# Interleaving the two halves of split weights: stationary operands at every second word

## The chip, the cores and the metric

One NeuronCore of a Trainium2 chip runs the whole kernel. The metric is the time of one execution on the device in microseconds. A profile of one execution lies beside it: each instruction's start and recorded duration by engine, the DMA transfers, and the clock that TensorE was granted.

## The reference, cut to what matters

One encoder layer over 256 tokens of width 2048, in fp32:

```
hn   = rmsnorm(x) * norm_w
q, v, f_fwd, f_bwd, z_a, b_gate, c_gate, h_b, z_b = split(hn @ w_in, 9)   # 2048 -> 9 x 2048
o_a  = head_rmsnorm(hgrn2_bidirectional(silu(q), v, f_fwd, f_bwd)) * silu(z_a)
o_b  = rmsnorm(b_gate * conv3(c_gate * h_b)) * silu(z_b)
h    = x + concat(o_a, o_b) @ w_out                                       # 4096 -> 2048
h    = h + (p @ w_ple) * sigmoid(h @ w_ple_gate)
out  = rmsnorm(h) * final_norm_w
```

The change touches the first product alone, `hn @ w_in`, whose weights are 2048 x 18432.

## The kernel before, in words

**Exactness.** TensorE multiplies fp32r operands. To keep fp32 exactness each operand is split in two: `hi` is the value rounded to fp32r, `lo` is what is left of it. A product is then hi x hi + hi x lo + lo x hi, summed in PSUM.

**Weights.** `Stream` (from line 31) brings them in. A DMA on SP's queue fills a `raw` tile of 128 x 2048 words (three buffers), which makes two units of 1,024 words per partition. For each unit `open` (line 58) takes one of five `spl` tiles of 128 x 2048 words, and `split` (line 68) fills it in two instructions: ScalarE casts `raw` to `hi` (line 69), VectorE subtracts `hi` from `raw` and writes `lo` (line 70). In the tile the 256 `hi` words of a k-tile lie next to each other, and its 256 `lo` words behind them; the view `[partition, k, s, n]` names them with s = 0 for `hi` and s = 1 for `lo`. `get` (line 72) keeps three units split ahead of the one in use.

**The GEMM.** A block is 256 columns of `w_in` for all 16 k-tiles, four units of four k-tiles. There are 72 blocks. Stage A runs i = 0 to 7 over FF, FB, Q, ZA, V (line 523), with the recurrence of two heads between the matmuls; stage B runs i = 0 to 7 over CG, HB, BG, ZB (line 547). ZA and V are token-major (16 blocks): x is the stationary operand, the weight the moving one. The other 56 are column-major: the weight is the stationary operand, x (`xs`) the moving one. For each k-tile and each half m of 128 columns `gemm_part` (line 272) issues a pair:

```
lh, ll = w[:, k, 0, m * P : (m + 1) * P], w[:, k, 1, m * P : (m + 1) * P]       # line 281
rf, rh = xs[:, kt, :, :].rearrange("p s n -> p (s n)"), xs[:, kt, 0, :]         # line 282
pe.matmul(a[:, :T], lhsT=ll, rhs=rh, start=False, stop=False)                   # line 287
pe.matmul(a, lhsT=lh, rhs=rf, start=False, stop=(kt == NKT - 1))                # line 288
```

The first takes `lo` of the weight as stationary operand and moves 256 columns, the second takes `hi` and moves 512 (for the first k-tile the two come the other way round, lines 284 and 285). So a block is 32 pairs, and each matmul has its own load of 128 stationary columns. After a block `evac` (line 297) adds the two halves of the accumulator, ScalarE at line 307 and VectorE at line 308; accumulators lie in four PSUM buffers, two for a block.

**Order.** Each engine takes its instructions in program order. The first two blocks (FF and FB of i = 0) have an order written out by hand (from line 317); behind them the tile framework orders the engines, and `at`/`tick` (lines 212 to 221) put the recurrence's matmuls (lines 459, 501, 511, 512) between k-tiles.

Of the kernel before, what the change touches and what calls it, by code (L numbers as in the profile page):

```python
# [25 lines left out]
B_Q, B_V, B_FF, B_FB, B_ZA, B_BG, B_CG, B_HB, B_ZB = (8 * i for i in range(9))  # L26
# [4 lines left out]
class Stream:  # L31


    def __init__(self, nc, rawp, splp, ahead):
        self.nc, self.rawp, self.splp, self.ahead = nc, rawp, splp, ahead
        self.todo = []
        self.where = []
        self.raws = {}
        self.parts = {}
        self.next = 0  # L40

    def add(self, src):

        j = len(self.todo)
        _, k, n = src.shape
        self.todo.append((src, k, n))
        first = len(self.where)
        self.where += [(j, h) for h in range(k * n // 1024)]
        return list(range(first, len(self.where)))
# [8 lines left out]
    def open(self, i):  # L58
        j, h = self.where[i]
        n = self.todo[j][2]  # L60
        if j not in self.raws:
            self.load(j)
        half = self.raws[j][:, h * 1024 : (h + 1) * 1024].rearrange("p (k n) -> p k n", n=n)
        part = self.splp.tile([P, 2048], F32R, tag="spl", name=f"spl{i}")
        self.parts[i] = part.rearrange("p (k s n) -> p k s n", s=2, n=n)
        return half, self.parts[i]

    def split(self, r, v):
# [12 lines left out]
def tile_hymba_encoder(  # L81
# [33 lines left out]
    ws = Stream(nc, rawp, splp, 3)  # L115

    blocks = {}
    for i in range(8):
        for c in (B_FF, B_FB, B_Q, B_ZA, B_V):
            blocks[c, i] = sum((ws.add(w_in[c + i, h]) for h in range(2)), [])  # L120
    for i in range(8):
        for c in (B_CG, B_HB, B_BG, B_ZB):
            blocks[c, i] = sum((ws.add(w_in[c + i, h]) for h in range(2)), [])
    oblocks = [sum((ws.add(w_out[j, h]) for h in range(8)), []) for j in range(4)]
    gblocks, pblocks = [], []
    for j, (c0, n) in enumerate(GCOLS):
# [660 lines left out]
```

## Time and profile before

| | |
|---|---|
| median of 3 runs | 1158.66 us (1158.42 to 1159.83) |
| the profiled execution | 1158.74 us |
| its span, first to last instruction | 1157.0 us |
| TensorE: matmul busy, weight loads busy | 1142.3 us, 981.4 us |
| VectorE, ScalarE, GpSimd busy | 763.6, 639.9, 234.8 us |
| mean granted TensorE clock | 0.995 of full |
| read from HBM | 211.11 MB |

In the profile PE is TensorE's matmuls and PEld its weight loads, which overlap the matmuls; DVE is VectorE, ACT is ScalarE, POOL is GpSimd, SP the queue that issues the DMAs. A group of instructions is named by line, engine, operation and tiles, out<-in, with the count after x. Recorded durations of successive matmuls overlap, so that their starts tell more than their durations.

### The profile page before, as it was taken

The numbers are of one execution on the slowest core, as the hardware profiler recorded it, in microseconds if no ns is written. First come the engines' busy times: TensorE is split into PE (matmuls) and PEld (weight loads), VectorE is DVE, ScalarE is ACT, GpSimd is POOL, SyncE is SP. The second block draws the span as 40 slices with busy tenths as digits, with TensorE's granted clock in tenths as the row PEclk, the third lists the DMA queues.
The fourth block names the chain that finished last, engine by engine and source line by source line (L and its number), as shares of the span: only waits on it lengthen the run. The fifth ranks groups of instructions, "written<-read, shape, count | busy, mean of one in ns | idle before, by whom it ended". The sixth has DMA issues, their size and how long they took to land.

```text
span 1157.0 us, 16851 instructions
## 1 busy us (share of the span) xinstructions
PE 1142.3 (99%) x6832; PEld 981.4 (85%) x6832; DVE 763.6 (66%) x949; ACT 639.9 (55%) x889; POOL 234.8 (20%) x167
## 2 busy tenths in 40 slices
PE   8999999999999999999999999999999999999997
PEld 7878888888888888888888888888888888888886
DVE  6687777685958585966666666676666545545554
ACT  6767576666758584855544444444444334434554
POOL 1232414151414041331221221121210000000121
PEclk9999999999999999999999999999999999999999
DMA  8754545454544555455555555555557555555541
GB/s 284 301 175 153 183 163 196 152 183 146 198 167 159 174 177 181 152 178 182 183 187 184 198 191 187 182 182 184 187 190 262 183 198 180 191 204 196 197 166 74
DMA packets 31614, 214.29 MB, mean 185 GB/s; under 512 B 3504, under 2 KB 3888, under 8 KB 7088
## 3 DMA queue, kind: packets, MB, share of 16 engines
q1 hardware_dynamic: 31392, 213.14, 53.6%
q8 instruction: 53, 0.87, 0.3%
q14 instruction: 25, 0.20, 0.1%
q10 hardware_dynamic: 144, 0.08, 0.0%
HBM read 211.11 MB, written 2.10 MB: 184 GB/s over the span
## 4 chain that ended last, share of the span: by engine, by line
PE 93%; DVE 2%; DMA 2%; POOL 1%; ACT 1%; SPq 0%; issue 0%; ACTq 0%; DVEq 0%
PE a L288 41%; PE a L287 21%; PE a L284 3%; PE pa L630 3%; PE pb L630 3%; PE pb L631 3%; PE pb L632 3%; PE pa L631 3%; PE pa L632 3%; PE pg L630 3%; PE pg L631 3%; PE pg L632 3%; PE a L285 1%; DVE spl L70 1%; PE scps L459 1%; PE cx L501 1%
## 5 line engine op out<-in xcount | busy, mean ns | idle before, releaser
L70 DVE TENSOR_TENSOR spl<-raw,spl 128x1024 fp32r<-128x1024 f32 (+1 forms) x389 | 522.3, 1348 | 305.9 <-ACT spl L69 304.9
L288 PE MATMUL a<-xs,spl 128*128 128x512 f32 x1680 | 597.2, 398 | 0.0
L69 ACT CAST spl<-raw 128x1024 fp32r<-128x1024 f32 (+1 forms) x389 | 405.0, 1045 | 343.0 <-PE a L288 193.7
L287 PE MATMUL a<-xs,spl 128*128 128x256 f32 x1680 | 476.0, 283 | 0.5 <-DVE spl L70 0.3
L288 PEld LDWEIGHTS a<-xs,spl 128*128 128x128 f32 x1680 | 316.7, 189 | 73.0
L287 PEld LDWEIGHTS a<-xs,spl 128*128 128x128 f32 x1680 | 318.1, 189 | 3.7 <-DVE spl L70 1.3
L288 PE MATMUL a<-spl,xs 128*128 128x512 f32 x480 | 171.4, 401 | 2.2 <-DVE spl L70 2.2
L287 PE MATMUL a<-spl,xs 128*128 128x256 f32 x480 | 135.4, 282 | 0.0
L288 PEld LDWEIGHTS a<-spl,xs 128*128 128x128 f32 x480 | 91.0, 190 | 24.1 <-DVE spl L70 2.5
L287 PEld LDWEIGHTS a<-spl,xs 128*128 128x128 f32 x480 | 91.4, 190 | 0.7
L307 ACT COPY r<-a 128x256 f32<-128x256 f32 x112 | 40.6, 372 | 47.4 <-PE a L288 46.8
L691 POOL TENSOR_TENSOR hh<-hh,fw 128x512 f32<-128x512 f32 (+1 forms) x10 | 12.8, 1293 | 264.5 <-PE pp L632 245.0
L630 PE MATMUL pg<-spl,ht 128*128 128x512 f32 (+1 forms) x160 | 55.7, 348 | 0.0
L632 PE MATMUL pg<-spl,ht 128*128 128x512 f32 (+1 forms) x160 | 55.5, 347 | 0.0
L631 PE MATMUL pg<-spl,ht 128*128 128x512 f32 (+1 forms) x160 | 55.5, 347 | 0.0
L630 PE MATMUL pa<-spl,mixa 128*128 128x512 f32 x128 | 51.2, 400 | 0.0
L438 POOL TENSOR_TENSOR qc<-pf,ge 128x256 f32<-128x256 f32 x16 | 43.9, 2748 | 34.4 <-DVE pf L430 34.4
L631 PE MATMUL pb<-spl,mixb 128*128 128x512 f32 x128 | 50.6, 395 | 0.0
L630 PE MATMUL pb<-spl,mixb 128*128 128x512 f32 x128 | 50.6, 395 | 0.0
L632 PE MATMUL pb<-spl,mixb 128*128 128x512 f32 x128 | 50.6, 395 | 0.0
L631 PE MATMUL pa<-spl,mixa 128*128 128x512 f32 x128 | 50.6, 395 | 0.0
L632 PE MATMUL pa<-spl,mixa 128*128 128x512 f32 x128 | 50.6, 395 | 0.0
(174 smaller groups left out, 1233.7 us busy)
## 6 DMA issues: line engine op xcount, KB each, us to landing
raw<-in_w_in_dram SPq DMA_DIRECT2D x140, 1024.0 KB, 5.0
raw<-in_w_out_dram SPq DMA_DIRECT2D x32, 1024.0 KB, 4.9
raw<-in_w_gate_dram SPq DMA_DIRECT2D x12, 1024.0 KB, 4.9
raw<-in_w_gate_end_dram SPq DMA_DIRECT2D x4, 1024.0 KB, 4.9
raw<-in_w_in_dram SPq DMA_DIRECT2D x7, 512.0 KB, 8.4
xf<-in_xtok_dram SPq DMA_DIRECT2D x1, 2048.0 KB, 9.9
hh<-in_xtok_dram SPq DMA_DIRECT2D x1, 2048.0 KB, 8.8
raw<-in_w_ple_dram SPq DMA_DIRECT2D x4, 512.0 KB, 3.5
```

The source lines that it names most:

```text
L69: self.nc.scalar.copy(out=v[:, :, 0, :], in_=r)
L70: self.nc.vector.tensor_tensor(out=v[:, :, 1, :], in0=r, in1=v[:, :, 0, :], op=ALU.subtract)
L284: pe.matmul(a, lhsT=lh, rhs=rf, start=True, stop=False)
L285: pe.matmul(a[:, :T], lhsT=ll, rhs=rh, start=False, stop=False)
L287: pe.matmul(a[:, :T], lhsT=ll, rhs=rh, start=False, stop=False)
L288: pe.matmul(a, lhsT=lh, rhs=rf, start=False, stop=(kt == NKT - 1))
L307: act.copy(out=r, in_=acc[m][:, 1, :])
L438: pool.tensor_tensor(out=c64(dst[:, d]), in0=c64(src[:, d, :, half * P : (half + 1) * P]), in1=g.unsqueeze(3).broadcast_to([P, 2, 2, CH]), ...
L630: pe.matmul(acc[m], lhsT=lh, rhs=w[:, k, 0, :], start=(kt == 0), stop=False)
L631: pe.matmul(acc[m], lhsT=lh, rhs=w[:, k, 1, :], start=False, stop=False)
L632: pe.matmul(acc[m], lhsT=ll, rhs=w[:, k, 0, :], start=False, stop=(kt == nk - 1))
L691: pool.tensor_tensor(out=h, in0=h, in1=fw[:, cs], op=ALU.mult)
```

## The change

The units of 23 blocks are laid out otherwise in their `spl` tile: `hi` and `lo` of each weight lie side by side, so that a view of `hi` alone, or of `lo` alone, steps by two words (8 bytes). These are FB for i = 1 to 7 and HB and ZB for all i, all of them column-major. The instructions and their order stay; ScalarE writes `hi` at this step, VectorE reads `hi` and writes `lo` at it, and TensorE loads its stationary operands at it.

```diff
     def __init__(self, nc, rawp, splp, ahead):
...
+        self.side = []
...
-    def add(self, src):
+    def add(self, src, side=False):
...
         self.todo.append((src, k, n))
+        self.side.append(side)
...
     def open(self, i):
...
         part = self.splp.tile([P, 2048], F32R, tag="spl", name=f"spl{i}")
-        self.parts[i] = part.rearrange("p (k s n) -> p k s n", s=2, n=n)
+        form = "p (k n s) -> p k s n" if self.side[j] else "p (k s n) -> p k s n"
+        self.parts[i] = part.rearrange(form, s=2, n=n)
...
     for i in range(8):
         for c in (B_FF, B_FB, B_Q, B_ZA, B_V):
-            blocks[c, i] = sum((ws.add(w_in[c + i, h]) for h in range(2)), [])
+            blocks[c, i] = sum((ws.add(w_in[c + i, h], c == B_FB and i > 0) for h in range(2)), [])
     for i in range(8):
         for c in (B_CG, B_HB, B_BG, B_ZB):
-            blocks[c, i] = sum((ws.add(w_in[c + i, h]) for h in range(2)), [])
+            blocks[c, i] = sum((ws.add(w_in[c + i, h], c in (B_HB, B_ZB)) for h in range(2)), [])
```

## Rows read from the trace of the kernel before

**Rows 1.** The page: busy time of each engine, and TensorE's clock by slices.
```profile
PE 1142.3 (99%) x6832; PEld 981.4 (85%) x6832; DVE 763.6 (66%) x949; ACT 639.9 (55%) x889; POOL 234.8 (20%) x167
...
PEclk9999999999999999999999999999999999999999
```

**Rows 2.** Waits of TensorE for the GEMM: us in total, times, longest.
```profile
PE a L288 <- DVE spl L70: 2.2, 1, 2.2
...
PE a L287 <- DVE spl L70: 0.3, 1, 0.3
```

**Rows 3.** The page: the chain that ended last, by engine, by line.
```profile
PE 93%; DVE 2%; DMA 2%; POOL 1%; ACT 1%; SPq 0%; issue 0%; ACTq 0%; DVEq 0%
PE a L288 41%; PE a L287 21%; PE a L284 3%; PE pa L630 3%; PE pb L630 3%; PE pb L631 3%; PE pb L632 3%; PE pa L631 3%; PE pa L632 3%; PE pg L630 3%; PE pg L631 3%; PE pg L632 3%; PE a L285 1%; DVE spl L70 1%; PE scps L459 1%; PE cx L501 1%
```

**Rows 4.** Column-major groups by form: busy us, mean ns | idle before.
```profile
L288 PE MATMUL a<-xs,spl 128*128 128x512 f32 x1680 | 597.2, 398 | 0.0
...
L287 PE MATMUL a<-xs,spl 128*128 128x256 f32 x1680 | 476.0, 283 | 0.5 <-DVE spl L70 0.3
...
L287 PEld LDWEIGHTS a<-xs,spl 128*128 128x128 f32 x1680 | 318.1, 189 | 3.7 <-DVE spl L70 1.3
L288 PEld LDWEIGHTS a<-xs,spl 128*128 128x128 f32 x1680 | 316.7, 189 | 73.0
```

**Rows 5.** Timeline of TensorE in ZB, i = 1: start us, us, what.
```profile
585.11 0.28 PE L287 MATMUL a<-xs,spl 128*128 128x256 f32 x1
...
586.52 0.28 PE L287 MATMUL a<-xs,spl 128*128 128x256 f32 x1
586.64 0.40 PE L288 MATMUL a<-xs,spl 128*128 128x512 f32 x1
586.88 0.28 PE L287 MATMUL a<-xs,spl 128*128 128x256 f32 x1
...
591.82 0.28 PE L287 MATMUL a<-xs,spl 128*128 128x256 f32 x1
...
594.30 0.28 PE L287 MATMUL a<-xs,spl 128*128 128x256 f32 x1
```

**Rows 6.** Weight loads by form: the recurrence's loads of 32 columns.
```profile
L459 PEld LDWEIGHTS scps<-pf,dd 128*32 128x32 f32 x384 | 10.4, 109 | 0.0
```

**Rows 7.** Timeline of weight loads: six in a row between short matmuls.
```profile
216.85 0.19 PEld L512 LDWEIGHTS o<-vt,sx 128*128 128x128 f32 x1
...
217.40 0.19 PEld L287 LDWEIGHTS a<-xs,spl 128*128 128x128 f32 x1
```

**Rows 8.** Timeline of TensorE in CG, i = 1.
```profile
550.39 0.28 PE L287 MATMUL a<-xs,spl 128*128 128x256 f32 x1
...
560.45 0.28 PE L287 MATMUL a<-xs,spl 128*128 128x256 f32 x1
```

**Rows 9.** The split's two groups, by form.
```profile
L70 DVE TENSOR_TENSOR spl<-raw,spl 128x1024 fp32r<-128x1024 f32 x387 | 520.9, 1352 | 304.8 <-ACT spl L69 303.7
L69 ACT CAST spl<-raw 128x1024 fp32r<-128x1024 f32 x387 | 403.8, 1047 | 341.8 <-PE a L288 193.7 <-PE pb L632 56.1 <-PE pa L632 47.1
```

**Rows 10.** Small VectorE groups: stepped operands (line 422), contiguous ones (199).
```profile
L422 DVE TENSOR_TENSOR gx<-dd,pf 128x6 f32<-128x6 f32 x8 | 1.3, 159 | 0.0
...
L199 DVE TENSOR_TENSOR et<-vec,mx 128x32 f32<-128x32 f32 x2 | 0.3, 190 | 0.0
```

**Rows 11.** Stage B by window: us, busy PE, PEld, DVE, ACT, POOL, clock, DMA.
```profile
600.00:700.00 100.00, 100.00 (x569) 86.92 (x568) 65.40 (x73) 46.92 (x61) 20.24 (x14) 1.00 0.56 189
```

**Rows 12.** Timeline, both engines of one split for ZB, i = 1.
```profile
580.74 1.05 ACT L69 CAST spl<-raw 128x1024 fp32r<-128x1024 f32 x1 [1.77 <-PE a L288]
...
581.82 1.23 DVE L70 TENSOR_TENSOR spl<-raw,spl 128x1024 fp32r<-128x1024 f32 x1 [1.60 <-ACT spl L69]
```

**Rows 13.** The page: DMA issues, KB each, median us to landing.
```profile
raw<-in_w_in_dram SPq DMA_DIRECT2D x140, 1024.0 KB, 5.0
```

## Prediction

> **What bounds the kernel now.** I read the busy shares first. TensorE has a matmul in flight 99% of the span, and its granted clock is at the full level (2.4 GHz) in practically every slice; VectorE and ScalarE are busy 66% and 55% [rows 1]. A busy TensorE does not yet prove that TensorE is the limit, so the waits come next: in the whole span the longest wait of a matmul of this GEMM for a split is 2.2 us, once, and the next is 0.3 us [rows 2]. The chain of waits says the same: 93% of it is TensorE, and 62 points of that are the two matmul lines 287 and 288 [rows 3]. What counts, then, is not how busy anything is, but how far apart two matmuls start. That is read from a timeline of TensorE alone, because the recorded durations overlap: a 512-column matmul is recorded with 398 ns and a 256-column one with 283 ns [rows 4], but the first starts of 27 successive pairs in ZB, i = 1, a block that the change touches, lie 594.30 - 585.11 = 9.19 us apart, 26 steps of 0.353 us [rows 5]. Within a pair the 256-column matmul holds the array for 0.12 us and the 512-column one for 0.23 to 0.24 us [rows 5]. The weight load of each matmul (189 ns recorded, [rows 4]) starts with the matmul before it and so lies beside that one.
>
> So the place to look at is the 0.12 us of the 256-column matmul: the load of the next `hi` operand has to fit in there.
>
> **The change part by part.**
>
> *How much is touched.* Side by side are FB for i = 1 to 7 (7 blocks) and HB and ZB for i = 0 to 7 (16): 23 of the 56 column-major blocks, 23 of all 72. A block is 16 k-tiles x 2 halves = 32 pairs, so 736 pairs, that is 1,472 weight loads at a step of 8 bytes, and 23 x 4 = 92 splits. Instruction counts, DMAs, queues, the order of the work and all semaphores stay as they are; nothing is added or moved.
>
> *Weight loads.* No row of the trace has a stationary operand with a step, so the cost is bounded from both sides. The low end is zero. For the high end I take that every column takes twice as long to come in. What a column costs follows from two rows: a load of 128 columns takes 189 ns [rows 4], one of 32 columns 109 ns [rows 6], so 96 columns take 80 ns, 0.83 ns each, 107 ns for 128, and 82 ns are fixed. How closely loads can follow each other is seen where short matmuls leave nothing else to wait for: six loads in a row, the first at 216.85 and the last at 217.40 with two merged rows of two between them, are 0.55 / 5 = 0.11 us apart [rows 7]. Under the 256-column matmul (0.12 us) there is thus about 0.01 us to spare, under the 512-column one 0.12 us. Twice the time per column adds 0.107 us: under the 512-column matmul it stays hidden (0.22 against 0.23), under the 256-column one 0.10 us of it comes out. High end: 736 x 0.10 = 74 us.
> Between 0 and 74 us I take zero, by the row that is nearest. While the loads bring in a column each 0.83 ns, the moving operand, of the same fp32r type and out of SBUF too, is read at 512 columns in 0.235 us [rows 5], 0.46 ns each. A load at every second word spans 256 words in 107 ns, 0.42 ns for each word passed over: the pace at which the moving operand already passes over its words. Reading past every second word asks of the memory about what the engine gets from it for the other operand.
> The Trainium skill has a price for this, SBUF — State Buffer, section "Door 1: The DMA port swizzle" (its box on cachelines): lines of 16 bytes, full bandwidth from two hits in a line on. At 8 bytes a line is hit twice instead of four times, so the sum by that page is 0 us as well; no run here shows it yet, and two hits is the least that it allows.
>
> *A gain from the loads.* This is not excluded either, since the same pair runs at two paces in this trace: in CG, i = 1, 29 steps from pair to pair take 560.45 - 550.39 = 10.06 us, 0.347 us a pair [rows 8], with the same shapes, the same clock and the same operands' layout as the 0.353 us of [rows 5]. If the new loads tipped all 736 pairs to the quicker pace, it would be 736 x 0.0066 = 4.9 us. In the other direction, the longest steps of [rows 5] (0.12 and 0.24 us) for every pair would be 0.36, 736 x 0.0065 = 4.8 us more. I take neither: 0.
>
> *Splits.* ScalarE writes 1,024 values with a step, VectorE reads one operand and writes its result with a step. Today they take 1,047 and 1,352 ns in the mean [rows 9]. The only rows with a stepped operand on VectorE are small: six values at a step of 256 bytes take 159 ns, 32 contiguous ones 190 ns [rows 10], 26 values more for 31 ns; so the step makes no value visibly dearer, though six are few. Bounds: nothing, and twice the present time. I take nothing; and up to the high end it is covered. In 100 us of stage B VectorE works 65.4 us and ScalarE 46.9 us [rows 11]; 100 us hold 35 units of 2.83 us, half of them side by side, so twice the time adds 17.7 x 1.23 = 22 us and 17.7 x 1.05 = 19 us: 87 and 66 us, still below 100. The cover that hides the latency is the lead: the split that ends on VectorE at 583.05 [rows 12] is first used by the matmul at 591.82 [rows 5], 8.8 us later. ScalarE started it right after a matmul of line 288 gave its buffer free [rows 12], so the lead comes from the five buffers, and a chain slower by 1.05 + 1.23 us leaves 6.5 us of it. Queued behind the longer splits on these engines are the evacuations (lines 307, 308); an accumulator is wanted again one block, some 11 us, after its last matmul, so a few us of delay there stop nobody. Behind VectorE's splits waits SP's queue too, which loads a `raw` tile again once both its halves are split; three tiles are six units, 17 us, and a transfer lands after 5.0 us [rows 13], so 1.23 us more are covered there as well. If the cover were gone, TensorE would wait at the first matmul of a unit.
>
> *Sum.* 0 + 0 + 0. The profiled execution took 1158.74 us (span 1157.0 and 1.7 around it), 0.1 us above the median of the runs, so I predict **1158.7 us**. A measurement of this kernel tells about 0.2% (2.3 us) from no change.
>
> **Rivals.**
> 1. *The stepped load is slower* (the other side). Place: the load under the 256-column matmul, 736 times. It decides from 0.01 us on, 12 columns' worth. At twice the time per column +74 us, **1232 us**; at one and a half times 0.053 - 0.01 = 0.043 us x 736, +32 us, **1190 us**. For it: the cover there is nearly used up already, and no row shows such a load. Against it: the pace of the moving operand. Chance 0.15, two thirds of it near the high price. The same box of the skill's page says that each access that crosses to a new line pays a penalty, without a figure; taken alone, that sentence would speak for this rival.
> 2. *The pairs fall into another pace.* For it: 0.347 and 0.353 us stand side by side for equal work [rows 5, 8], so the pace hangs on something fine, which the load's timing could be. Quicker: -4.9 us, **1153.8 us**, chance 0.14. Slower: +4.8 us, **1163.5 us**, chance 0.06. Against both: 0.353 us is the common pace; 569 matmuls in 100 us of stage B [rows 11] are 0.352 us a pair.
> 3. *The splits outgrow their cover.* Stage B has 100 - 65.4 = 34.6 us of VectorE left per 17.7 units, so a split may grow by 1.95 us to about 3.2 us; only past that does VectorE set the pace. At three times today's time (2.46 us more) it would be 0.5 us for each of the 92 splits, 47 us, **1206 us**. For it: nothing seen. Chance 0.03.
>
> **How the numbers follow.** No visible effect 0.62. Faster is rival 2's quick half, 0.14. Slower is 0.15 + 0.06 + 0.03 = 0.24. From 1153.5 to 1164.5 us lie the forecast and both halves of rival 2, 0.82; left out are rivals 1 and 3.
>
> **What would show it.** Right: pairs in HB and ZB at 0.353 us as in CG and BG, loads still near 189 ns, no more waits of TensorE for splits than now. Wrong by rival 1: loads of lines 284 to 288 longer in the touched blocks alone, and the step after a 256-column matmul 0.2 us instead of 0.12. By rival 2: touched blocks at another length than their neighbours with loads unchanged. By rival 3: long splits, and TensorE waiting for line 70 in stage B. If ScalarE's or VectorE's splits grow and the time does not, the cover was as reckoned.

## The result, and the profile after

| | before | changed |
|---|---|---|
| median | 1159.24 us (1158.42 to 1160.18) | 1153.59 us (1152.67 to 1154.78) |
| ratio | | 0.9949 [0.9936, 0.9961] |
| the profiled execution | 1158.74 us, span 1157.0 us | 1154.37 us, span 1152.7 us |
| mean granted clock | 0.995 | 0.996 |

Both medians are over four runs. The changed kernel is faster by 0.51%. The forecast was no visible effect, 1158.7 us: the gain was missed, and the measured time lies just inside the lower edge of the range (1153.5 us). In the changed kernel every line behind the inserted ones has a number 4 higher: the pair is 291 and 292, the split 73 and 74.

The page of the changed kernel, with the rows that answer to [rows 1, 3]: busy time, clock, chain.

```profile
PE 1136.3 (99%) x6832; PEld 985.1 (85%) x6832; DVE 762.6 (66%) x949; ACT 647.7 (56%) x889; POOL 235.0 (20%) x167
...
PEclk9999999999999999999999999999999999999998
...
PE 93%; DVE 2%; DMA 2%; POOL 1%; ACT 1%; SPq 0%; issue 0%; ACTq 0%; DVEq 0%
```

The page says where to look, and no more: the count of instructions is the same, TensorE still bounds the kernel with the same 93% of the chain, and its matmuls are busy 6.0 us less. Its waits for splits, as in [rows 2]:

```profile
PE a L292 <- DVE spl L74: 2.7, 1, 2.7
...
PE a L291 <- DVE spl L74: 0.3, 1, 0.3
```

No wait went away: the two are as they were, one of them 0.5 us longer. So 5 us were not won from a stall; the matmuls themselves follow each other faster. The groups by form, as in [rows 4, 9]:

```profile
L292 PE MATMUL a<-xs,spl 128*128 128x512 f32 x1680 | 591.9, 395 | 0.0
L74 DVE TENSOR_TENSOR spl<-raw,spl 128x1024 fp32r<-128x1024 f32 x387 | 519.9, 1349 | 307.1 <-ACT spl L73 306.2
L291 PE MATMUL a<-xs,spl 128*128 128x256 f32 x1680 | 474.5, 282 | 0.4 <-DVE spl L74 0.3
L73 ACT CAST spl<-raw 128x1024 fp32r<-128x1024 f32 x387 | 412.1, 1069 | 335.5 <-PE a L292 173.8 <-PE pb L636 56.1 <-PE pa L636 47.4
L291 PEld LDWEIGHTS a<-xs,spl 128*128 128x128 f32 x1680 | 322.7, 192 | 3.3 <-DVE spl L74 1.0
L292 PEld LDWEIGHTS a<-xs,spl 128*128 128x128 f32 x1680 | 321.2, 191 | 63.7
```

The loads went up by 2 to 3 ns in the mean, the matmuls down by 1 to 3 ns, and ScalarE's casts up by 22 ns. A mean over touched and untouched blocks hides what each does. (Touched blocks are the 23 with side-by-side units; a load at the step of 8 bytes is called stepped below.) So the next view is the loads of one touched block alone, ZB of i = 1 (583 to 593 us):

```profile
L292 PEld LDWEIGHTS a<-xs,spl 128*128 128x128 f32 x30 | 5.9, 195 | 1.0
L291 PEld LDWEIGHTS a<-xs,spl 128*128 128x128 f32 x29 | 5.7, 196 | 0.0
```

and of the untouched block ahead of it, BG of i = 1 (572 to 582 us):

```profile
L291 PEld LDWEIGHTS a<-xs,spl 128*128 128x128 f32 x29 | 5.4, 188 | 0.0
L292 PEld LDWEIGHTS a<-xs,spl 128*128 128x128 f32 x29 | 5.4, 188 | 1.3
```

A stepped load takes 7 to 8 ns more. The kernel got faster with dearer loads. The timeline of TensorE shows where: the start of stage B's second round, the two blocks just named with their first and last pairs, and the first matmul behind the GEMM.

```profile
548.70 0.40 PE L288 MATMUL a<-xs,spl 128*128 128x512 f32 x1
...
571.02 0.40 PE L288 MATMUL a<-xs,spl 128*128 128x512 f32 x1
...
571.73 0.28 PE L291 MATMUL a<-xs,spl 128*128 128x256 f32 x1
...
581.78 0.28 PE L291 MATMUL a<-xs,spl 128*128 128x256 f32 x1
...
582.13 0.39 PE L288 MATMUL a<-xs,spl 128*128 128x512 f32 x1
...
583.19 0.28 PE L291 MATMUL a<-xs,spl 128*128 128x256 f32 x1
583.31 0.40 PE L292 MATMUL a<-xs,spl 128*128 128x512 f32 x1
583.54 0.28 PE L291 MATMUL a<-xs,spl 128*128 128x256 f32 x1
...
592.99 0.28 PE L291 MATMUL a<-xs,spl 128*128 128x256 f32 x1
593.34 0.40 PE L288 MATMUL a<-xs,spl 128*128 128x512 f32 x1
...
861.99 0.48 PE L634 MATMUL pa<-spl,mixa 128*128 128x512 f32 x1
```

The touched block runs 28 steps in 592.99 - 583.19 = 9.80 us, 0.350 us a pair, where the same block took 0.353 [rows 5]. The untouched block runs 29 steps in 581.78 - 571.73 = 10.05 us, 0.347 us a pair: the quicker of the two paces that were there before [rows 5, 8].

K-tile by k-tile the start times show what a pace is. A quick block takes 0.693 to 0.694 us for each k-tile, two pairs. At the slow pace the k-tiles take about 0.715, 0.704 and 0.701 us in turn, so that 0.353 us is the mean of a pattern of three k-tiles. The touched blocks take 0.700 us for each. A block of Q, ZA or stage B (i from 1 on) has one pace from its fourth k-tile on. In an unstepped one the second k-tile already tells which: 0.711 to 0.712 us in all that go on slowly, 0.698 to 0.700 us in all that go on quickly, in both traces. So in these two kernels the pace of a block is settled at its start.

Two points of the kernel before enclose the same stretch (timeline of TensorE, CG of i = 1 and the first matmul behind the GEMM):

```profile
549.69 0.40 PE L284 MATMUL a<-xs,spl 128*128 128x512 f32 x1
...
866.34 0.48 PE L630 MATMUL pa<-spl,mixa 128*128 128x512 f32 x1
```

866.34 - 549.69 = 316.65 us before, 861.99 - 548.70 = 313.29 us after: 3.36 us won over 28 blocks. From block start to block start in the two timelines, each of the 14 touched ones (HB and ZB) is 0.07 to 0.08 us shorter and each of 13 untouched ones (CG and BG) 0.18 us; the fourteenth, CG of i = 1, had the quick pace already [rows 8]. 14 x 0.075 + 13 x 0.18 = 3.4 us. Over all 72 blocks the touched ones won 1.34 us (FB 0.24, HB 0.63, ZB 0.47) and the untouched ones 4.2 us (Q 1.27, ZA 0.51, CG 0.99, BG 1.44); the start of the kernel (the first two blocks, V of i = 0 and FF of i = 1) took 1.2 us more, which makes 4.36 us. Q and CG (from i = 1 on) and every BG stand directly behind a touched block. ZA does not: it follows Q, and only ZA of i = 2, 4 and 6 won. Behind the GEMM both take 290.7 us. **Three quarters of the gain lie in blocks that the change doesn't touch.**

A count of matmuls in 100 us of stage B serves for the experiments; the columns are those of [rows 11], where it is 569:

```profile
600.00:700.00 100.00, 100.00 (x575) 88.73 (x574) 66.17 (x73) 49.32 (x62) 18.97 (x14) 1.00 0.56 189
```

### The profile page after: what moved, and what is told of

Read it like the earlier page. It is cut to its first block, busy times and chain, and to the rows that moved or that the text cites. A ratio compares the mean times of both kernels' runs of the same rounds, so it can differ in the third digit from the quotient of the medians.

```text
span 1152.7 us, 16851 instructions
## 1 busy us (share of the span) xinstructions
PE 1136.3 (99%) x6832; PEld 985.1 (85%) x6832; DVE 762.6 (66%) x949; ACT 647.7 (56%) x889; POOL 235.0 (20%) x167
## 4 chain that ended last, share of the span: by engine, by line
PE 93%; DVE 2%; DMA 2%; POOL 1%; ACT 1%; SPq 0%; issue 0%; ACTq 0%; DVEq 0%
PE a L292 40%; PE a L291 21%; PE a L288 3%; PE pa L634 3%; PE pb L636 3%; PE pb L634 3%; PE pa L636 3%; PE pb L635 3%; PE pa L635 3%; PE pg L636 3%; PE pg L635 3%; PE pg L634 3%; PE a L289 1%; PE scps L463 1%; DVE spl L74 1%; PE cx L505 1%
## 5 line engine op out<-in xcount | busy, mean ns | idle before, releaser
L73 ACT CAST spl<-raw 128x1024 fp32r<-128x1024 f32 (+1 forms) x389 | 413.3, 1066 | 335.8 <-PE a L292 173.8
L292 PEld LDWEIGHTS a<-xs,spl 128*128 128x128 f32 x1680 | 321.2, 191 | 63.7
L291 PEld LDWEIGHTS a<-xs,spl 128*128 128x128 f32 x1680 | 322.7, 192 | 3.3 <-DVE spl L74 1.0
```

Of the source, the lines that this page charges most:

```text
L73: self.nc.scalar.copy(out=v[:, :, 0, :], in_=r)
```

## The experiments

### Loads or splits: which half of the change does it

Each kernel steps one side alone, in the change's 23 blocks. In the first, the tiles are written without a step and read with one:

```diff
 # e1_loads, in open()
-        return half, self.parts[i]
+        return half, part.rearrange("p (k s n) -> p k s n", s=2, n=n)
 # e2_writes, in open(); self.parts[i] keeps the old form
-        return half, self.parts[i]
+        return half, part.rearrange(form, s=2, n=n)
```

> Loads stepped, splits contiguous, in the same 23 blocks (the touched stationary operands mix hi and lo words, so the product of these blocks is another one). Theory P (the stepped loads shift the phase between loads and matmuls, and a block entered in another phase runs at 0.347 us a pair instead of 0.353): as the changed kernel, 1153.6 us, with CG and BG at 10.88 us from first to last matmul start. Rival W (the stepped writes of ScalarE and VectorE do it, by their own timing or their traffic): as before, 1159.2 us, CG and BG at 11.05 us.

> Splits stepped, loads contiguous, in the same 23 blocks (the touched stationary operands mix hi and lo words, so the product of these blocks is another one). Theory P: as before, 1159.2 us, CG and BG at 11.05 us, loads at 189 ns. Rival W: as the changed kernel, 1153.6 us, CG and BG at 10.88 us.

Stepped loads alone: 1153.88 us (1152.59 to 1154.38), ratio 0.9944 [0.9931, 0.9957]. Stepped splits alone: 1159.38 us (1157.72 to 1160.78), 0.9996 [0.9987, 1.0004]. The windows of stage B, first of the kernel with stepped loads:

```profile
600.00:700.00 100.00, 100.00 (x575) 88.71 (x574) 66.37 (x73) 47.80 (x62) 18.93 (x14) 1.00 0.55 189
```

then of the one with stepped splits:

```profile
600.00:700.00 100.00, 100.00 (x569) 86.91 (x568) 65.61 (x73) 48.81 (x61) 19.23 (x14) 1.00 0.56 190
```

575 matmuls as in the changed kernel, and 569 as before: the loads make the whole effect, the splits none of it.

### Only the last unit of each touched block

The change's 23 blocks, but of the four units of a block only the last is stepped.

```diff
-        self.parts[i] = part.rearrange("p (k s n) -> p k s n", s=2, n=n)
+        form = "p (k n s) -> p k s n" if self.side[j] and h == 1 else "p (k s n) -> p k s n"
+        self.parts[i] = part.rearrange(form, s=2, n=n)
...
+ ... ws.add(w_in[c + i, h], c == B_FB and i > 0 and h == 1) ...
+ ... ws.add(w_in[c + i, h], c in (B_HB, B_ZB) and h == 1) ...
```

> Only the last of the four units of each of the 23 blocks has hi and lo side by side. Theory P: what the next, untouched block enters from is still a stepped unit, so Q, CG and BG keep 10.88 us (about 4.4 us of the 5.6 us gained), and the touched blocks go back to nearly 11.05 us: 1154.9 us. Rival S (every stepped load saves time itself, so the gain goes with their number): a quarter of 5.6 us, 1157.8 us, CG and BG at 11.05 us.

1156.69 us (1155.03 to 1157.41), 0.9971 [0.996, 0.9982]: between the two expected times. The blocks tell more than the total. Each CG and BG that stands behind a stepped unit is 0.16 to 0.17 us shorter (but for CG of i = 1, which was quick before), each Q of i = 1 to 7 0.18, nearly as in the changed kernel; HB and ZB are as before (0.00 to 0.01), three quarters of their pairs being unstepped and the rest too few to show; ZA stays too. So the loads of four k-tiles at the end of a block suffice to change the block behind it. Q, CG and BG won 3.5 us here, against 3.7 us in the changed kernel, with a quarter of the stepped loads; the 1.34 us of the touched blocks and the 0.5 us of ZA are gone, and the start took 1.1 us more than before.

### Every column-major block stepped

54 blocks (all but the first FF and FB) in place of 23.

```diff
+ ... ws.add(w_in[c + i, h], c in (B_FB, B_FF, B_Q) and (i > 0 or c == B_Q)) ...
+ ... ws.add(w_in[c + i, h], True) ...
```

> hi and lo side by side in all column-major blocks but FF and FB of i = 0 (54 instead of 23). Theory P: a stepped block runs at 10.98 us in stage B wherever it stands, so CG and BG lose their 10.88 us, HB and ZB keep 10.98 us, and of the token-major blocks ZA, entered from a stepped Q, runs at 10.88: about 4.8 us less than before, 1154.6 us, no better than the change. Rival S (each stepped load saves time itself): 54/23 of the gain of 5.6 us, 1146 us.

1158.23 us (1156.78 to 1159.57), 0.999 [0.9981, 0.9999]: nearly the time before, so both theories missed. Its window of stage B:

```profile
600.00:700.00 100.00, 100.00 (x567) 89.17 (x566) 64.23 (x72) 50.30 (x61) 19.97 (x14) 1.00 0.56 189
```

In stage B a stepped block behind another stepped one takes 0.03 us more than before, 0.354 us a pair, while the unstepped ZA and V behind a stepped Q win 0.17 to 0.19 us each. Stepped FB blocks win 0.10 us each: FB of i = 2 runs from its fourth to its eleventh k-tile at 0.693 to 0.694 us, the quick pace, and slowly behind the recurrence's matmuls. This ends the idea that a stepped load is by itself the better one, and also that a stepped block has a pace of its own. **Stepped loads helped most in an unstepped block behind them**, and the gain of the change hangs on having such blocks. It is not the only way to the quick pace: V in this kernel and ZA of i = 2, 4 and 6 in the changed one win behind unstepped blocks, and the next experiment has no stepped load at all.

### No step at all: the order of the pair

The kernel before has one irregular place in every block: the first k-tile issues its pairs 512 then 256 columns, all others 256 then 512. Here every k-tile has the order of the first, and nothing is stepped.

```diff
-                if kt == 0:
...
+                pe.matmul(a, lhsT=lh, rhs=rf, start=(kt == 0), stop=False)
+                pe.matmul(a[:, :T], lhsT=ll, rhs=rh, start=False, stop=(kt == NKT - 1))
```

> No step anywhere: the kernel before, but the pair has the same order in every k-tile (512 columns with hi, then 256 with lo), so that no block boundary interrupts the alternation. Theory P: the pace in force goes on over the boundaries; FF leaves the recurrence's matmuls at 0.347 us a pair, so the blocks behind it keep 0.347 us: some 55 blocks x 0.2 us less, about 1148 us. If instead the slow pace is what the alternation always falls into, 1159 us or up to 1160. Rivals S and W: no stepped load or write, so 1159.2 us.

> The kernel with one order once more, to catch the trace of an execution at its other time (two of six took 1147 us, four 1154 us, at the same granted clock). Theory P: an execution at 1154 us has all of stage B from CG of i = 1 on at 0.353 us a pair, one at 1147 us at 0.347: 31 blocks x 32 pairs x 0.0066 = 6.5 us of the 7.2 us between them. Against it: the 7.2 us lie in the start or in single waits.

> The kernel with one order a third time, for the trace of an execution at 1154 us. Theory P: if this one takes 1154 us, its stage B runs at 0.353 us a pair from CG of i = 1 to ZB of i = 7; if it takes 1147 us, at 0.347 us. Against it: 1154 us with stage B at 0.347.

Six runs of the first: 1147.0, 1154.09, 1153.98, 1154.73, 1154.15, 1146.86 us (ratio by the median 0.993 [0.9907, 0.9953]); the same program once more 1147.25 and once more 1155.38 us. The expectation had one time, 1148 us or 1159 us; there are two. The mean granted clock is 0.995 to 0.997 in all of them, and nothing lies between the two times. Windows of the execution of 1147.0 us, two of stage A and two of stage B:

```profile
140.00:240.00 100.00, 100.00 (x699) 87.84 (x698) 74.34 (x103) 69.06 (x105) 26.02 (x16) 1.00 0.47 161
240.00:340.00 100.00, 100.00 (x736) 87.75 (x735) 70.51 (x94) 64.17 (x100) 30.44 (x19) 1.00 0.54 180
540.00:640.00 100.00, 100.00 (x579) 87.44 (x578) 66.39 (x75) 48.72 (x63) 21.20 (x14) 1.00 0.55 189
640.00:740.00 100.00, 100.00 (x578) 87.44 (x578) 66.97 (x74) 46.85 (x61) 18.93 (x13) 1.00 0.57 192
```

and of the one of 1155.38 us:

```profile
140.00:240.00 100.00, 100.00 (x698) 88.03 (x697) 73.82 (x102) 67.88 (x103) 25.13 (x15) 1.00 0.49 166
240.00:340.00 100.00, 100.00 (x736) 87.97 (x735) 71.07 (x92) 64.03 (x100) 31.33 (x19) 1.00 0.53 179
540.00:640.00 100.00, 100.00 (x568) 86.77 (x568) 65.36 (x74) 48.70 (x63) 19.06 (x13) 1.00 0.56 189
640.00:740.00 100.00, 100.00 (x568) 86.77 (x567) 65.39 (x75) 46.44 (x61) 20.79 (x14) 1.00 0.55 183
```

These windows of stage A are alike, to one matmul; in stage B one has 579 matmuls in 100 us and the other 568. 200 / 579 = 0.345 and 200 / 568 = 0.352 us a pair: the two paces (0.347 and 0.353 from block start to block start), each held from CG of i = 1 to the end of stage B, in one and the same program. That stretch takes 311.42 and 317.39 us, 5.97 of the 8.4 us between the two executions, where 6.5 of 7.2 us were expected; the other 2.4 us lie ahead of it. So here a pace goes on over block boundaries until something disturbs it. The irregular first k-tile, which is missing here, is the nearest candidate for that. In the kernel with stepped last units, HB of i = 2 comes out of a quick CG, its first k-tiles take 0.693, 0.712, 0.690 and 0.715 us, and it is slow from there on; here no such place stands between CG and HB, and HB stays quick. It doesn't always act so: in the changed kernel ZA of i = 2 stays quick behind a quick Q.

### Does a stepped unit set the pace

The order of the last experiment, with stepped last units in FB (i from 1 on), HB and ZB of i = 0 only.

```diff
+ ... ws.add(w_in[c + i, h], c in (B_HB, B_ZB) and h == 1 and i == 0) ...
```

> One order of the pair in every k-tile, and one stepped unit (the last) in FB of i = 1 to 7 and in HB and ZB of i = 0, nowhere else. Theory P: a block entered from a stepped unit runs at 0.347 us a pair, and without a break at the block boundaries it keeps that pace, so that every execution comes out at the lower of the two times of the kernel with one order: 1147 us, spread under 2 us. If a stepped unit does not settle the pace there: again two times, 1147 and 1154 us. Rival S: 9 stepped units of 92, so 0.6 us of the gain on top of the kernel with one order alone, 1153.5 us in the median.

1154.53 us (1154.24 to 1155.12), 0.996 [0.9947, 0.9972], and 568 matmuls in each of the windows 540 to 640 and 640 to 740 us. The expectation missed: with no irregular k-tile behind it, a stepped unit doesn't bring the quick pace. The persistence shows here too: from the middle of ZB of i = 0 on, which is ahead of that block's stepped unit, the profiled execution holds the slow pace through stage B, and all five runs lie near the longer time of the last experiment.

### Other orders

The order changes inside each k-tile (512, 256 for the first half, 256, 512 for the second), or from k-tile to k-tile; nothing is stepped.

```diff
 # e8_flip
-                if kt == 0:
+                if kt == 0 or m == 0:
 # e10_kt_flip
-                if kt == 0:
+                if kt % 2 == 0:
 # both: the 512-column matmul of this branch, then the 256-column one
+ ... start=(kt == 0), stop=False)
+ ... start=False, stop=(kt == NKT - 1))
```

> No step anywhere: the kernel before, but in every k-tile the first half's pair goes 512 then 256 columns and the second half's 256 then 512, so the alternation is broken in every k-tile instead of once a block. Theory P2 (what keeps the slow pace is an undisturbed alternation of equal loads; any regular break, by the order or by a stepped load, lets the fast pace come back): about 0.347 us a pair in all blocks, 1147 to 1149 us in every execution. Rival B (the break at a block's start is what throws a fast block back into the slow pace): every k-tile slow or slower, 1159 us or more.

> No step: both pairs of an even k-tile go 512 then 256 columns, both pairs of an odd one 256 then 512, so the alternation is broken once a k-tile, half as often as in the kernel with the flip between the halves (348.6 ns a pair, 1151.1 us). Theory P2 (a regular break keeps the slow pace from settling, and each break has a small price of its own): between 0.347 and 0.349 us a pair, 1148 to 1151 us in every execution. Rival: a stretch of two pairs is long enough for the slow pace to come back, 0.351 us and more, 1155 us or above.

Inside a k-tile: 1151.06 us (1150.69 to 1152.73), 0.9931 [0.9918, 0.9945]; far from rival B's 1159 us, but above the 1147 to 1149 us of theory P2, at 0.349 us a pair. From k-tile to k-tile: 1153.47 us (1153.42 to 1154.79), 0.9954 [0.994, 0.9967]; here the expectation missed, it fell between its two cases. The window of the first:

```profile
600.00:700.00 100.00, 100.00 (x576) 87.35 (x575) 65.43 (x72) 46.65 (x60) 18.92 (x13) 1.00 0.56 190
```

576 matmuls in 100 us, and 574 in the same window of the other: with frequent changes of order neither falls to the 568 of the slow pace, and neither falls into two groups of times 7 us apart in five runs. The first is, by its median, the best of the versions that hold one time, 2.5 us below the changed kernel, with neither a stepped load nor a new layout; the intervals of the two ratios overlap a little (0.9918 to 0.9945 against 0.9936 to 0.9961), so that this last difference is likely rather than sure.

### Twice the step

In the 23 blocks the words of a k-tile are read at a step of 16 bytes: the stationary views take every fourth word.

```diff
+        v = part.rearrange("p (k s n) -> p k s n", s=2, n=n)
+        self.parts[i] = part.rearrange("p (k n s) -> p k s n", s=4, n=128) if self.side[j] else v
+        return half, v
...
+                    if w.shape[2] == 4:
+                        lh, ll = w[:, k, m, :], w[:, k, 2 + m, :]
```

> Splits contiguous, the loads of the same 23 blocks at every fourth word, 16 bytes (the touched stationary operands mix hi and lo words, so the product of these blocks is another one). At 8 bytes a load took 196 ns instead of 188. If the price goes with the words passed over, 16 bytes cost two to three times those 8 ns: loads near 205 to 212 ns, the step after a 256-column matmul 0.13 us, touched blocks 11.3 to 11.6 us, some 1160 to 1165 us. If a load that meets each 16-byte line once only is served at half the rate (the Trainium skill's rule on lines, read with the numbers of this trace): loads near 296 ns, that step 0.22 us, 1230 us.

1245.25 us (1244.45 and 1246.06), 1.0741 [1.0721, 1.0761]. Loads of one touched block (597 to 611 us):

```profile
L294 PEld LDWEIGHTS a<-xs,spl 128*128 128x128 f32 x30 | 10.0, 335 | 0.0
L295 PEld LDWEIGHTS a<-xs,spl 128*128 128x128 f32 x30 | 9.3, 311 | 0.0
```

and the timeline of TensorE in it:

```profile
600.04 0.28 PE L294 MATMUL a<-xs,spl 128*128 128x256 f32 x1
600.16 0.51 PE L295 MATMUL a<-xs,spl 128*128 128x512 f32 x1
600.51 0.28 PE L294 MATMUL a<-xs,spl 128*128 128x256 f32 x1
600.63 0.51 PE L295 MATMUL a<-xs,spl 128*128 128x512 f32 x1
```

A pair takes 600.51 - 600.04 = 0.47 us: two loads at 0.235 us each, back to back, against 0.11 us in [rows 7]. The loads are the bound of these blocks now. 736 x (0.47 - 0.353) = 86 us, which is the 86 us measured. Of the two expected times the nearer is the 1230 us of the rule on lines, 15 us too low: the loads were expected at 296 ns, and the longer step behind the 256-column matmul. Block by block the touched ones take 88.6 us more, and Q, CG and BG behind them 4.0 us less, 0.19 to 0.20 us each from i = 2 on: the quick pace behind a stepped block once more. Against this the 8-byte step costs 7 to 8 ns of a load.

### Another suspect: where the tiles lie

In the last stage the 512-column matmuls on `pa` and `pb` start 233 ns apart and those on `pg` 227 ns. To see whether the place of the stationary operand of `pa` and `pb` (`mixa` and `mixb`) does it, 96 unused bytes behind `mixa` are meant to put both tiles at multiples of 64 bytes.

```diff
+    mixp.tile([P, 24], F32, name="pad")
```

> The kernel before with 96 unused bytes behind mixa, so that mixa and mixb, the stationary operands of the output projection, start at a multiple of 64 bytes like xs, ht and spl, and not 32 bytes off. In the kernel before the 512-column matmuls of pa and pb start 233.3 ns apart, those of pg, with the same order and the same moving tiles but ht as the stationary operand, 226.8 ns. If the place of the stationary operand is what sets the pace there: pa and pb at 226.8 ns, 768 x 6.5 ns = 5 us less, 1154.3 us. Rival (a matter of phase alone): pa and pb stay at 233.3 ns or land on either, 1159.3 us.

1157.16 us (1155.9 to 1158.89), 0.9982 [0.9974, 0.9991]; `pa` and `pb` still 233 ns. So this shift leaves that step as it was. Most of the small gain stands in Q, 0.19 us in each of i = 1 to 7: one more case of another pace, from an edit that changes neither the loads' step nor the order.

## Why the prediction was wrong

**What bounds the kernel: right.** TensorE's start-to-start step decided, and no wait did.

**A gain from the loads: the step that failed.** It read the two paces, 0.347 and 0.353 us, said that the pace "hangs on something fine, which the load's timing could be", priced the tip at 4.9 us, and then took "neither: 0". A zero needs something that holds the slow pace in place. There was no such row; that 0.353 us was the common pace showed only what the old loads led to. The load's length then changed by 7 to 8 ns, more than the 6.6 ns between the paces. Where the prediction has 0, the runs show 1.34 us won in the touched blocks and 4.2 us in untouched ones, and the kernel with stepped loads alone shows that the loads do it.

**Rival 2: right in sign and size, wrong in place.** Its quick half gave 1153.8 us at a chance of 0.14, measured 1153.59 us. But it multiplied the step by the 736 touched pairs. Those won 1.34 us, about a quarter of that 4.9, at 0.350 us a pair in place of 0.347; the quick pace came to untouched blocks, most of them behind the touched ones, which the sum had no term for. That the size agreed is luck: 4.2 us from a place that was left out stand beside 1.34 us from the one that was counted. The sign by which the prediction would have known this rival, "touched blocks at another length than their neighbours with loads unchanged", was half wrong as well: the lengths differ, and the loads did change.

**The price of the stepped load: right at the step used.** The prediction's bounds were 0 and 74 us, taken at 0; the load grew by 7 to 8 ns, and the touched pairs still got shorter, 0.350 us against 0.353. Stepped FB blocks ran at 0.347 us a pair for part of their way, so a stepped load doesn't rule out the quick pace. The prediction's argument from the moving operand's pace came to the right side; no run tests it by itself.
The Trainium skill, SBUF — State Buffer, section "Door 1: The DMA port swizzle" (its box on cachelines), would have two hits in a line of 16 bytes for full bandwidth. The traces agree nearly: two hits cost 7 to 8 ns of 188, and one hit (16-byte step) doubles the spacing, 0.11 to 0.235 us.

**Rival 1 did not occur, and its place was drawn wrongly.** It put an exposed load under the 256-column matmul, as the whole prediction did ("the place to look at"). Where loads really are the bound, at the 16-byte step, the step behind the 256-column matmul stays 0.12 us and the one behind the 512-column one grows to 0.35 us [rows 5 for 0.24]. The sum for a pair was near enough: 0.10 us reckoned for a load twice as slow per column, 0.117 us measured at 16 bytes.

**The splits: right.** ScalarE's timeline in stage B has the four stepped casts for ZB of i = 1 and the first unstepped one behind them:

```profile
571.49 1.12 ACT L73 CAST spl<-raw 128x1024 fp32r<-128x1024 f32 x1
574.01 1.15 ACT L73 CAST spl<-raw 128x1024 fp32r<-128x1024 f32 x1 [1.40 <-PE a L292]
576.78 1.18 ACT L73 CAST spl<-raw 128x1024 fp32r<-128x1024 f32 x1 [1.63 <-PE a L292]
579.55 1.11 ACT L73 CAST spl<-raw 128x1024 fp32r<-128x1024 f32 x1 [1.60 <-PE a L292]
...
582.60 1.05 ACT L73 CAST spl<-raw 128x1024 fp32r<-128x1024 f32 x1
```

1.14 us in the mean against 1.05 us, some 90 ns more. VectorE's subtractions show no rise: 1,349 ns in the mean, and in HB and ZB 1.40 to 1.43 us in both traces. The waits for splits above are as before: the lead covers the 90 ns many times over, and the kernel with stepped splits alone took the time before. The prediction's bound took 1.23 us for a split on VectorE, the figure of one row; with the 1.35 us of [rows 9] twice the time adds 24 us and not 22, 89 us of 100, still covered.

**Shown, and open.** Shown: the loads cause the gain, not the splits; untouched blocks take most of it; with every column-major block stepped it is nearly gone; the order of the pair alone gives as much and more; one program can hold either pace. Not shown is what in the engine makes the two paces stable, and which event picks one: the expectations on that missed, in whole or in part. Stretches at half clock (1.2 GHz) at the kernel's start are no simple answer, since of the two executions near 1147 us that were profiled one has two such stretches and the other none. Why `pa` and `pb` run at 233 ns and `pg` at 227 ns stays open as well.

## What to carry to other kernels

When TensorE is 99% busy with nothing to wait for, divide a block by its pairs and look for the same pair at two paces: if there are two, an edit that changes a load by a few ns, or the order of a pair, can move the kernel by half a per cent in blocks that it doesn't touch, so give such a tip a real chance and sum it over all blocks. Before crediting a layout for such a gain, try the cheap rival that has no layout in it, here the order of two matmuls, and apply the edit everywhere: a real saving adds up, a change of pace does not. A stationary operand at a step of 8 bytes cost this kernel nothing; at 16 bytes the loads followed each other at twice the distance and became the bound.

## What the runs showed of the hardware that was not expected

- Pairs of equal matmuls at the full clock have two paces, 0.347 and 0.353 us, and can keep one for some 300 us. One program, unchanged, took 1147 or 1154 to 1155 us; in the two traces compared, 6 of the 8.4 us between them are the pace of stage B.
- The pace of an unstepped block of Q, ZA or stage B shows in its second k-tile, 0.698 to 0.700 us or 0.711 to 0.712 in the traces before and after, and holds to the block's end.
- Loads that are 7 to 8 ns longer in one block go with a next, untouched block that is 0.18 us shorter.
- Loads at a 16-byte step follow each other at 0.235 us where contiguous ones did at 0.11, and the time comes out behind the longer of the two matmuls, not behind the shorter.
- ScalarE's cast of 1,024 values writes with an 8-byte step in 1.11 to 1.18 us where it took 1.05.
